# Six trial write-backs on GpSimd between the first tile and the second in a nanmax over 65536 rows

## The chip, the core and the metric

The kernel runs on one core of one Trainium2 chip. The metric is the device time of one execution in microseconds (us). Before the change it is 1251.34 us, the median of 3 runs (1251.2 to 1251.43).

Engines are named as in the profile: DVE is VectorE, ACT is ScalarE, POOL is GpSimd, SP is SyncE, which here only issues DMAs. TensorE does nothing.

## The reference

```python
def setup_inputs():
    batch, seq, dim = 32, 2048, 2048
    x = np.random.randn(batch, seq, dim).astype(np.float32)
    mask = np.random.rand(batch, seq, dim) < 0.1
    x[mask] = np.nan
    return {"x": x, "axis": -1}

def reference(x, axis):
    return np.nanmax(x, axis=axis).astype(np.float32)
```

512 MiB of float32 with a tenth of NaNs are read, and the largest number of each of the 65536 rows of 2048 elements is written, 256 KiB in all.

## The kernel before, in words

The maximum of a row must pass over NaNs. The kernel does that on the upper 16 bits of each number, before DVE takes an ordinary maximum:

1. **Load.** SP loads a tile of up to seven rows for each of the 128 partitions (up to 128x14336 elements, 7 MiB) into one of three buffers `xt` (L469; the very first load is L264).
2. **Key.** ACT reads the upper half of each float as an int16, and writes a 16-bit key for it into one of three buffers `kt` of 6144 elements (L277). The key saturates, so that NaNs come out as an ordinary pattern of a very small number.
3. **Write-back.** POOL (in the later part of the program at times ACT) turns the key back and writes it over the upper half in `xt`: `key * -1 + TOP` by one `tensor_scalar` with two operations, a packed uint16 source and an int16 target of stride two (L287).
4. **Maximum.** DVE reduces the cleaned rows of the tile to one number each (L294).

At five places POOL also looks for rows in which every element was a NaN (L309 and L323), and at the end SP stores the results (L556).

A table, `TILES`, gives for each of the 74 tiles how it is cut in loads, keys, write-backs and maxima, in units of 512 elements. The first tile, number 0, has one row for each partition (4 units, 128x2048). The next 46 have 28 units: one load, keys and write-backs of 7, 9 and 12 units, maxima of 16 and 12 units. Tile *n* uses buffer `xt[n % 3]`, and its load waits until DVE has finished tile *n* - 3. Keys go round through the buffers `kt[1]`, `kt[2]`, `kt[0]`, and so on: tile 0's key and the first key of tile 1 share `kt[1]`, the second key of tile 1 is the first use of `kt[2]`, and the third the first use of `kt[0]`.

No scheduler moves anything. The instructions stand on each engine in the order in which the Python loop issues them, and each engine works in that order. `Order.add` gives each instruction the semaphore waits for the events that it is handed, without those that are already implied, and returns its own event. `kfree[k]` holds, for each key buffer, the last write-back that read it; a key into that buffer waits for it. For tiles listed in `EARLY`, the last key of the tile waits for the next buffer's write-backs too.

In the rows of the two programs below, `kt_60`, `kt_61` and `kt_62` are `kt[0]`, `kt[1]` and `kt[2]`; `xt` is the first buffer of rows, `xt_58` and `xt_59` are the other two.

Of the kernel before, what the change touches and what calls it, by code (L numbers as in the profile page):

```python
# [9 lines left out]
D = 2048  # L10
# [73 lines left out]
TOP = 0x7F7F  # L84
# [8 lines left out]
def joints(keys, backs, reds):  # L93


    parts = []
    pieces = []
    at = end = step = 0
    for n, wait in backs:
        end += n  # L100
        while at < end:
            at += keys[step]
            step += 1
        if wait is None or wait >= 0:
            parts.append((end - n, end, wait is not None, step + (wait or 0), len(pieces)))
        pieces.append(n)
    needs = []
    done = 0
    for n in map(abs, reds):
        over = [i for i, p in enumerate(parts) if p[0] < done + n and p[1] > done]  # L110
        done += n
        pools = [i for i in over if not parts[i][2]]
        acts = sorted((i for i in over if parts[i][2]), key=lambda i: parts[i][3])
        if pools and acts and parts[pools[-1]][3] > parts[acts[-1]][3]:
            acts = []
        needs.append(pools[-1:] + acts[-1:])
    pairs = {}
    for need in needs:
        if len(need) == 2 and all(sum(i in n for n in needs) == 1 for i in need):
            both = tuple(parts[i][4] for i in need)  # L120
            for i in both:
                pairs[i] = both
    return pairs
# [62 lines left out]
def kernel(  # L186
# [15 lines left out]
    nc = tc.nc  # L202
    P = nc.NUM_PARTITIONS
    f32, i32 = mybir.dt.float32, mybir.dt.int32
    i16, u16 = mybir.dt.int16, mybir.dt.uint16
    ALU = mybir.AluOpType
# [29 lines left out]
    kts = [sing.tile([P, KEYS], u16, name=f"kt{i}") for i in range(NKEYS)]  # L236
# [21 lines left out]
    order = Order(nc)  # L258
    heads = []
    for number in range(HEADS):  # L260
        (c,) = TILES[number][0]
        gi, base = place[number]
        to = xts[number][:, 0 : c * Q]
        head = nc.sync.dma_start(  # L264
            out=dataclasses.replace(to, dep_tracking_offset=to.offset + P * WIDE * D),
            in_=groups[gi][0][:, base : base + c * Q],
# [4 lines left out]
    with tc.tile_critical() as section:  # L271

        def act(deps, pair=None, **kw):
            return order.add(
                "act",
                nc.scalar,
                lambda: nc.scalar.activation(**kw),  # L277
                deps,
                lane=pair,
                joint=pair is not None,  # L280
            )
# [51 lines left out]
        kfree = [{} for _ in range(NKEYS)]  # L333
# [45 lines left out]
        def freed(*ks):  # L379

            uses = [(back, then, e) for k in ks for back, ((_, then), e) in kfree[k].items()]
            counts = [e[1] for _, _, e in uses if e[0] == "pool"]
            deps = []
            for back, then, e in uses:
                if back == "act" and order.count["act"] >= then:
                    e = ("act", then)
                if back != "pool" or e[0] == "pool" or all(v < then for v in counts):
                    deps.append(e)
            return deps
# [39 lines left out]
        def find_part(i):  # L429
            gi, lo, hi = spans[i]  # L430
            first = groups[gi][2]
            acc = accs[:, first + lo : first + hi]
            deps = [done_at[PARTS[i][2]]]
            if PARTS[i][3] == "dve":
                ready[i] = find("dve", nc.vector, deps, acc, None)
            else:
                none = late[:, 0 : hi - lo]
                ready[i] = find("pool", nc.gpsimd, deps, acc, none)

        for number, (loads, chunks, reds) in enumerate(TILES):  # L440
            keys = [k for ks, _ in chunks for k in ks]
            fresh = {}
            step = 0
            for ks, bs in chunks:
                assert sum(ks) * Q <= KEYS
                assert sum(ks) == sum(b[0] if isinstance(b, tuple) else b for b in bs)
                fresh[step] = int(sum(ks) * Q)
                step += len(ks)
            backs = [b for _, bs in chunks for b in bs]
            backs = [b if isinstance(b, tuple) else (b, None) for b in backs]  # L450
            assert sum(loads) == sum(keys) == sum(b for b, _ in backs) == sum(map(abs, reds))
            pairs[number] = joints(keys, backs, reds)
            for i, part in enumerate(PARTS):
                if part[3] == number:
                    find_part(i)
            gi, base = place[number]
            xg = groups[gi][0]
            xt, before = xts[number % BUFS], free[number % BUFS]
            assert number < BUFS or state["tile"] > number - BUFS
            landed = []  # L460
            at = 0
            for c in loads:
                c = int(c * Q)
                e = order.add(
                    "sp",
                    nc.sync,
                    lambda: heads[number]
                    if number < HEADS
                    else nc.sync.dma_start(  # L469
                        out=xt[:, at : at + c], in_=xg[:, base + at : base + at + c]  # L470
                    ),
                    before + lanes[turn],
                    lane=f"load{turn}",
                    step=16,
                )
                lanes[turn] = [e]
                turn = (turn + 1) % LANES
                landed.append((at, at + c, e))
                at += c
            end = at  # L480
            at = lo = part = 0
            for step, c in enumerate(keys):
                c = int(c * Q)
                here = [l for a, b, l in landed if a < at + c and b > at]
                kold = []
                if used + fresh.get(step, 0) > KEYS:
                    key = (key + 1) % NKEYS
                    used = 0
                    assert all(h[3] != key for h in held)
                    assert all(q[2] != key for v in half.values() for q in v)  # L490
                    kold = freed(key, (key + 1) % NKEYS) if number in EARLY and at + c == end else freed(key)
                    kfree[key] = {}
                e_key = act(
                    kold + here,
                    out=kts[key][:, used : used + c],
                    in_=xt[:, at : at + c].bitcast(i16)[:, 1::2],
                    func=ACT.Prelu,
                    bias=EDGE,
                    scale=-1.0,
                    alpha=float(TOP - LOW) / (EDGE - NAN),  # L500
                )
                used += c
                at += c
                for h in held:
                    h[-1] -= 1
                for h in [h for h in held if h[-1] <= 0]:
                    held.remove(h)
                    write(*h[:-1], "act")
                while backs and lo + backs[0][0] * Q <= at:
                    n, wait = backs.pop(0)  # L510
                    n = int(n * Q)
                    kp = kts[key][:, used - (at - lo) : used - (at - lo) + n]
                    if wait is not None and wait > 0:
                        held.append([number, lo, lo + n, key, kp, e_key, part, wait])
                    else:
                        who = "pool" if wait is None else "act" if wait == 0 else "dve"
                        write(number, lo, lo + n, key, kp, e_key, part, who)
                    lo += n
                    part += 1
                if number == len(TILES) - 1 and at == end:  # L520
                    for h in held:
                        write(*h[:-1], "act")
                    held.clear()
                maxima(number)
            assert lo == end
        assert state["tile"] == len(TILES)
        for i, part in enumerate(PARTS):
            if not isinstance(part[3], int):
# [4 lines left out]
        n = len(whole)  # L533
# [73 lines left out]
```

## Time and profile before

| what | value |
|---|---|
| median of 3 runs | 1251.34 us |
| the profiled execution | 1251.19 us |
| its span | 1249.5 us |
| DVE busy | 1109.5 us, 184 instructions |
| ACT busy | 979.2 us, 285 instructions |
| POOL busy | 1160.0 us, 255 instructions |
| DMA queue of the loads busy | 99.5% of the span |

The span runs from the first to the last recorded instruction of the profiled execution; the time beside it includes some 1.7 us around it. Busy times of the engines overlap. For a queue of DMAs, busy is the share of the 16 DMA engines' time that its packets took. An idle time in brackets stands before the instruction that ended it, with the engine that released that instruction.

### The profile page before, as it was taken

To read this page: it belongs to the slowest core of one execution; us is meant where nothing else is said; L and a number is where in the kernel's file an instruction comes from. 1 tells how busy PE (TensorE), PEld (TensorE's weight loads), DVE (VectorE), ACT (ScalarE), POOL (GpSimd) and SP (SyncE) were. 2 spreads that over 40 slices of the span, in tenths; PEclk is the share of its full clock that TensorE was granted. 3 is DMA by queue.
4 is the path that set the end of the run, shared out by engine and by line. 5 is a ranking of instruction groups with operands and counts; after the bars stand their busy time and mean duration, and the time that the engine had idled before them with its cause. 6 is when DMAs were issued, how large, how long until landed. Compare 5 with 4: busy or idle time off the path is not lost.

```text
span 1249.5 us, 915 instructions
## 1 busy us (share of the span) xinstructions
DVE 1109.5 (89%) x184; ACT 979.2 (78%) x285; POOL 1160.0 (93%) x255
## 2 busy tenths in 40 slices
DVE  0888889888889888889888888988898999999999
ACT  3777777777777777777777777799877789999998
POOL 2999999999999999999999999967999988999988
DMA  9999999999999999999999999999999999999997
GB/s 415 441 428 424 441 441 435 417 441 441 435 426 432 441 439 431 422 441 441 433 428 431 441 439 431 422 441 441 435 426 432 441 435 432 424 435 427 431 426 316
DMA packets 16950, 537.19 MB, mean 430 GB/s; under 512 B 2608, under 2 KB 2608, under 8 KB 5296
## 3 DMA queue, kind: packets, MB, share of 16 engines
q1 hardware_dynamic: 16944, 537.14, 99.5%
q14 instruction: 6, 0.05, 0.0%
HBM read 536.87 MB, written 0.26 MB: 430 GB/s over the span
## 4 chain that ended last, share of the span: by engine, by line
POOL 37%; DVE 29%; DMA 25%; ACT 8%; issue 1%; SPq 0%
POOL xt L287 37%; DVE acc L294 29%; DMA xt<-in_x_dram 25%; ACT kt L277 7%; ACT xt L277 2%; POOL late L309 0%; POOL acc L323 0%; SPq L264 0%; SPq L469 0%; DVE acc L301 0%; SPq L602 0%; SPq L271 0%
## 5 line engine op out<-in xcount | busy, mean ns | idle before, releaser
L287 POOL TENSOR_SCALAR xt<-kt 128x3584 int16<-128x3584 uint16 (+12 forms) x240 | 1155.0, 4812 | 83.4 <-ACT kt L277 68.2
L294 DVE TENSOR_REDUCE acc<-xt 128x3 f32<-128x6144 f32 (+4 forms) x183 | 1109.3, 6115 | 137.6 <-POOL xt L287 130.7
L277 ACT ACTIVATE kt<-xt 128x3584 uint16<-128x3584 int16 (+11 forms) x251 | 913.8, 3677 | 263.2 <-DMA xt<-in_x_dram 224.8
L277 ACT ACTIVATE xt<-kt 128x512 int16<-128x512 uint16 (+10 forms) x32 | 67.8, 2117 | 0.7
L309 POOL TENSOR_SCALAR late<-acc 128x112 int32<-128x112 f32 (+1 forms) x5 | 2.8, 559 | 0.4
L323 POOL TENSOR_TENSOR acc<-acc,late 128x112 int32<-128x112 int32 (+1 forms) x5 | 2.0, 397 | 0.4
L277 ACT ACT_TABLE_LOAD x1 | 1.3, 1283 | 1.3 <-SPq L271 1.3
L329 POOL MEMSET scalars<- 128x1 f32 x1 | 0.1, 98 | 0.9 <-SPq L271 0.9
L588 POOL MEMSET const-float32-0.0<- 128x1 f32 x1 | 0.1, 99 | 0.2 <-issue 0.2
L277 ACT ACTIVATE scalars<-scalars 128x1 f32<-128x1 f32 x1 | 0.2, 202 | 0.0
L301 DVE SCALAR_TENSOR_TENSOR acc<-acc 128x7 f32<-128x7 f32 x1 | 0.2, 166 | 0.0
L588 POOL MEMSET const-bfloat16-1.0<- 128x1 bf16 x1 | 0.1, 102 | 0.0
L588 POOL MEMSET const-uint8-127<- 128x1 uint8 x1 | 0.1, 102 | 0.0
L588 POOL MEMSET const-float32-1.0<- 128x1 f32 x1 | 0.1, 99 | 0.0
## 6 DMA issues: line engine op xcount, KB each, us to landing
xt<-in_x_dram SPq DMA_DIRECT2D x62, 7168.0 KB, 22.6
xt<-in_x_dram SPq DMA_DIRECT2D x6, 1536.0 KB, 24.9
xt<-in_x_dram SPq DMA_DIRECT2D x2, 4096.0 KB, 19.8
xt<-in_x_dram SPq DMA_DIRECT2D x2, 3584.0 KB, 25.7
xt<-in_x_dram SPq DMA_DIRECT2D x2, 3072.0 KB, 26.7
xt<-in_x_dram SPq DMA_DIRECT2D x1, 5632.0 KB, 20.3
xt<-in_x_dram SPq DMA_DIRECT2D x2, 2816.0 KB, 24.9
xt<-in_x_dram SPq DMA_DIRECT2D x2, 2560.0 KB, 26.0
```

The source lines that it names most:

```text
L277: lambda: nc.scalar.activation(**kw),
L287: lambda: nc.gpsimd.tensor_scalar(**kw),
L294: return order.add("dve", nc.vector, lambda: do(**kw), deps)
L301: lambda: engine.scalar_tensor_tensor(out=acc, in0=acc, scalar=0.0, in1=acc, op0=ALU.mult, op1=ALU.add),
L309: lambda: engine.tensor_scalar(out=none, in0=acc, scalar1=LEAST, scalar2=float(0x00400000), op0=ALU.is_lt, op1=ALU.mult,),
L323: lambda: engine.tensor_tensor(out=bits, in0=bits, in1=none, op=ALU.add),
L329: e_top = order.add("pool", nc.gpsimd, lambda: nc.gpsimd.memset(top, EDGE), [])
L588: nc = _bacc.Bacc("TRN2", target_bir_lowering=False, num_devices=1)
```

## The change

Behind the code of tile 0, and so ahead of everything of tile 1 on ACT, POOL and DVE, it adds the following:

- a memset on DVE that fills all 6144 elements of `kt[0]` with the constant 1;
- six instructions on POOL, each over 1024 elements from `kt[0]`, each into one of three ranges of `kt[2]` in the pattern of a write-back (int16, stride two). The first and the fifth have the write-back's two operations. The second and the sixth copy int16 to int16, the third copies uint16 to int16, the fourth multiplies only. The first four read 1024 packed elements; the fifth and sixth read every second of 2048;
- a wait of the first trial for the memset, and of each further trial for the one before it;
- an entry for the last trial in `kfree[0]` and `kfree[2]`, so that the next key into each of these buffers waits for it.

What the trials write is never read: the keys of tile 1 go over it.

```diff
             assert lo == end
+            if number == 0:
+                n = D // 2
+                e = order.add("dve", nc.vector, lambda: nc.vector.memset(kts[0], 1), [])
+                packed = kts[0][:, 0:n]
+                apart = kts[0][:, n : 3 * n][:, 1::2]
+                kt = kts[2].bitcast(i16)
+                g = nc.gpsimd
+                kw = dict(op0=ALU.mult, op1=ALU.add, scalar1=-1.0, scalar2=float(TOP))
+                trials = (
+                    lambda to: g.tensor_scalar(out=to[:, 1::2], in0=packed, **kw),
+                    lambda to: g.tensor_copy(out=to[:, 1::2], in_=packed.bitcast(i16)),
+                    lambda to: g.tensor_copy(out=to[:, 1::2], in_=packed),
+                    lambda to: g.tensor_single_scalar(
+                        out=to[:, 1::2], in_=packed, scalar=-1.0, op=ALU.mult
+                    ),
+                    lambda to: g.tensor_scalar(out=to[:, 1::2], in0=apart, **kw),
+                    lambda to: g.tensor_copy(out=to[:, 1::2], in_=apart.bitcast(i16)),
+                )
+                deps = [e]
+                for i, trial in enumerate(trials):
+                    to = kt[:, 2 * n * (i % 3) : 2 * n * (i % 3 + 1)]
+                    e = order.add("pool", g, lambda: trial(to), deps)
+                    deps = [e]
+                kfree[0] = {"pool": ((0, 0), e)}
+                kfree[2] = {"pool": ((0, 0), e)}
         assert state["tile"] == len(TILES)
```

POOL's queue at its start, as the instructions stand there with their waits; `xt<-kt_61 128x2048` is the write-back of tile 0, and `xt_58` belongs to tile 1:

```order
 L329 MEMSET scalars 128x1
 L287 ISA
 L287 TENSOR_SCALAR xt<-kt_61 128x2048 [waits order_act]
+L535 TENSOR_SCALAR kt_62<-kt_60 128x1024 [waits order_dve]
+L536 COPY kt_62<-kt_60 128x1024 [waits order_pool]
+L537 CAST kt_62<-kt_60 128x1024 [waits order_pool]
+L538 TENSOR_SCALAR kt_62<-kt_60 128x1024 [waits order_pool]
+L541 TENSOR_SCALAR kt_62<-kt_60 128x1024 [waits order_pool]
+L542 COPY kt_62<-kt_60 128x1024 [waits order_pool]
 L287 TENSOR_SCALAR xt_58<-kt_61 128x3584 [waits order_act]
 L287 TENSOR_SCALAR xt_58<-kt_62 128x4608 [waits order_act]
```

The six trials stand between the write-back of tile 0 and the first of tile 1, and nothing else has moved on POOL.

ACT's queue at its start, with the keys of tile 0, of tile 1 (from `xt_58`) and the first of tile 2 (from `xt_59`):

```order
 L277 ACT_TABLE_LOAD
 L277 ACTIVATE scalars<-scalars 128x1 [waits order_pool]
 L277 ACTIVATE kt_61<-xt 128x2048 [waits order_load0]
 L277 ACTIVATE kt_61<-xt_58 128x3584 [waits order_load1]
-L277 ACTIVATE kt_62<-xt_58 128x4608
+L277 ACTIVATE kt_62<-xt_58 128x4608 [waits order_pool]
 L277 ACTIVATE kt_60<-xt_58 128x6144 [waits order_pool]
 L277 ACTIVATE kt_61<-xt_59 128x3584 [waits order_load2]
```

The second key of tile 1 had no wait and now waits for POOL, that is for the last trial. On DVE the memset stands between the maximum of tile 0 and the first of tile 1. SP's queue is the same in both.

## The prediction

> **What bounds the kernel now.** I read the page's totals first, to see which resource is full.
>
> ```profile
> span 1249.5 us, 915 instructions
> DVE 1109.5 (89%) x184; ACT 979.2 (78%) x285; POOL 1160.0 (93%) x255
> DMA  9999999999999999999999999999999999999997
> DMA packets 16950, 537.19 MB, mean 430 GB/s; under 512 B 2608, under 2 KB 2608, under 8 KB 5296
> q1 hardware_dynamic: 16944, 537.14, 99.5%
> ...
> xt<-in_x_dram SPq DMA_DIRECT2D x62, 7168.0 KB, 22.6
> ```
>
> Three engines are busy for 78 to 93%, but the queue of the loads is busy for 99.5% of the span. The 512 MiB of input come in one unbroken stream, and while it is unbroken no engine's lateness shows at the end. So the question about any added work is not how long it takes but whether it makes a load start so late that the stream runs dry. A gap there is paid in full: the last 180 us are one chain on DVE, which hangs on the loads' landing.
>
> ```profile
> 1032.66 22.16 DMA xt<-in_x_dram
> ...
> 1068.18 125.79 DVE acc L294 x32
> 1193.98 52.93 DVE acc L294 x24
> ```
>
> These pieces of the chain that ended last say it: a load, and (after one key and two write-backs) DVE to the end.
>
> Next I read the timeline of the first 75 us, where the change sits. Columns: start, duration, engine and operation, idle time before it.
>
> ```profile
> 7.49 2.46 POOL L287 TENSOR_SCALAR xt<-kt 128x2048 int16<-128x2048 uint16 x1 [6.02 <-ACT kt L277]
> 9.99 2.29 DVE L294 TENSOR_REDUCE acc<-xt 128x1 f32<-128x2048 f32 x1 [9.99 <-POOL xt L287]
> ...
> 22.37 7.12 ACT L277 ACTIVATE kt<-xt 128x3584 uint16<-128x3584 int16 x2 [14.96 <-DMA xt<-in_x_dram]
> 25.64 16.70 POOL L287 TENSOR_SCALAR xt<-kt 128x3584 int16<-128x3584 uint16 x3 [15.68 <-ACT kt L277]
> 29.84 5.32 ACT L277 ACTIVATE kt<-xt 128x6144 uint16<-128x6144 int16 x1 [0.35 <-POOL xt L287]
> 35.24 15.14 DVE L294 TENSOR_REDUCE acc<-xt 128x4 f32<-128x8192 f32 x2 [22.97 <-POOL xt L287]
> 39.28 7.12 ACT L277 ACTIVATE kt<-xt 128x3584 uint16<-128x3584 int16 x2 [4.11 <-DMA xt<-in_x_dram]
> ...
> 56.26 7.12 ACT L277 ACTIVATE kt<-xt 128x3584 uint16<-128x3584 int16 x2 [4.15 <-DMA xt<-in_x_dram]
> ...
> 73.16 3.19 ACT L277 ACTIVATE kt<-xt 128x3584 uint16<-128x3584 int16 x1 [4.08 <-DMA xt<-in_x_dram]
> ```
>
> The reader is to see two things. POOL sits idle for 15.68 us before 25.64: that is the hole into which the trials go. And ACT starts a new tile at 39.28, 56.26 and 73.16, each time released by a landing, so a full tile takes the stream about 16.94 us.
>
> Then the loads. SP issues the load of a tile when DVE has finished the tile three before it in the same buffer. The wait list of SP's queue and two looks at the timeline show this:
>
> ```profile
> SPq L469 <- DVE acc L294: 1151.4, 70, 37.8
> ```
>
> ```profile
> 12.30 0.33 SPq L469 DMA_DIRECT2D xt<-in_x_dram  x1
> ```
>
> ```profile
> 50.41 0.33 SPq L469 DMA_DIRECT2D xt<-in_x_dram  x1
> ```
>
> The load of tile 3 goes out at 12.30, right behind DVE's first reduce, and that of tile 4 at 50.41, behind the two reduces of tile 1 (35.24 + 15.14 = 50.38). At 50.41 the stream still has tile 3 to deliver until about 56.24, so the queue is 5.83 us ahead. A load also needs time of its own before its bytes flow. The first load of all, issued into an empty queue, gives that:
>
> ```profile
> L264 SPq DMA_DIRECT2D xt<-in_x_dram x1: 368/368/368, 0.7 to 0.7; - x1
> ...
> DMA to landing us min/median/max: 4.7/4.7/4.7
> ```
>
> It carries 1 MiB, which at the page's mean of 430 GB/s takes 2.44 us, so about 2.26 us of the 4.7 are fixed. **Tile 4's load may therefore be late by 5.83 - 2.26 = 3.57 us before the stream stops.** That is the cover.
>
> **The change part by part.** It removes nothing. It adds one memset of 6144 elements on DVE, six instructions on POOL in a chain, a wait of the first trial for DVE, and a wait of ACT's key into buffer 2 (4608 elements, tile 1) for the last trial. In before, that key follows the first one without a stop inside the 7.12 us. The key into buffer 0 already waits for a later POOL instruction. SP's queue and the DMAs get nothing new: the load of tile 3 waits for DVE's first reduce, which stands ahead of the memset. Behind DVE's memset stands the reduce of 35.24; behind the trials stands the write-back of 25.64; behind the waiting ACT key stand the third key of tile 1 and then tile 2's.
>
> For the durations I use the groups of instructions kept apart by shape (busy us and mean ns of one behind the first bar):
>
> ```profile
> L294 DVE TENSOR_REDUCE acc<-xt 128x3 f32<-128x6144 f32 x62 | 405.6, 6543 | 1.2 <-POOL xt L287 1.2
> L287 POOL TENSOR_SCALAR xt<-kt 128x6144 int16<-128x6144 uint16 x51 | 359.1, 7041 | 4.6 <-ACT kt L277 0.6
> ...
> L287 POOL TENSOR_SCALAR xt<-kt 128x3584 int16<-128x3584 uint16 x57 | 239.0, 4193 | 24.6 <-ACT kt L277 21.9
> ...
> L287 POOL TENSOR_SCALAR xt<-kt 128x1024 int16<-128x1024 uint16 x6 | 8.0, 1335 | 0.6 <-ACT kt L277 0.2
> ...
> L309 POOL TENSOR_SCALAR late<-acc 128x112 int32<-128x112 f32 x4 | 2.4, 591 | 0.3
> ...
> L323 POOL TENSOR_TENSOR acc<-acc,late 128x112 int32<-128x112 int32 x4 | 1.7, 421 | 0.3
> ...
> L309 POOL TENSOR_SCALAR late<-acc 128x57 int32<-128x57 f32 x1 | 0.4, 431 | 0.1
> L323 POOL TENSOR_TENSOR acc<-acc,late 128x57 int32<-128x57 int32 x1 | 0.3, 304 | 0.1
> ...
> L329 POOL MEMSET scalars<- 128x1 f32 x1 | 0.1, 98 | 0.9 <-SPq L271 0.9
> ```
>
> *The memset.* No row shows a memset of this size. Below it stands the 0.10 us of a 128x1 memset, above it the 6.54 us that DVE takes to pass through 6144 elements in a reduce. I take 6.54, the same engine and the same count. DVE is free from 9.99 + 2.29, and SP acts on that at 12.30; so the memset ends at 18.84 and the first trial starts at 18.89 (0.05 for the hand-over, as between 7.49 + 2.46 and 9.99).
>
> The Trainium skill (VectorE: DVE Perf Modes, section "Zero memsets can be issued as uint32 (trn2)") says that a memset takes one cycle per element whatever the dtype. By its 0.96 GHz that is an estimate of 6.4 us, and the sum would be 0.1 us lower; no row here shows one.
>
> *The trials.* Trial 1 is the write-back's own form and has a row: 1.335 us. Trial 5 is the same two operations from a source of stride two; I take the same, with nothing else in the rows to price the stride. The other four (copy, copy with a change of type, one multiplication, copy from a strided source) are forms that no row shows. The rows bound them. The write-back costs (7041 - 4193) / 2560 = 1.11 ns an element. L309, the same opcode with a compare and a multiplication, costs (591 - 431) / 55 = 2.91 ns an element and 0.27 us fixed. L323, an add of two tensors, costs (421 - 304) / 55 = 2.13 ns. So of three forms on POOL the multiply-and-add alone is quick, and everything else on this engine costs two to three times as much per element. At 1024 elements the ends are 1.34 us and 0.27 + 1024 x 2.91 / 1000 = 3.25 us. I take the upper end for these four, since they are not multiply-and-add and the dearer one-input row is the nearest that isn't.
>
> *The sum.* 2 x 1.335 + 4 x 3.25 = 15.67 us. Between two POOL instructions of which the second waits for the first lie 0.07 to 0.08 us (313.51 + 0.61 to 314.19, below), five times, so 0.40. The last trial ends at 18.89 + 15.67 + 0.40 = 34.96, and the first write-back of tile 1 starts at 35.04 in place of 25.64: **9.40 us late**. The ACT key that now waits starts at 35.0 and takes 4 us (4608 of the 8192 elements in 7.12 us), about as long as the write-back beside it, so it adds nothing of its own. Everything behind keeps its spacing, and tile 4's load goes out at 59.81. Of the 9.40 us the cover takes 3.57; **5.83 us of empty stream are left**.
>
> What follows that? Not a second gap, but not by much: POOL, behind its work, makes a tile in 16.80 us (324.37 to 341.17 below), so tile 5's load goes out at 50.41 + 9.40 + 16.80 = 76.61 and can flow at 78.87, while tile 4 lands at 73.1 + 5.8 = 78.9. From then on POOL gains 0.14 us a tile on the stream. That lateness inside the cover costs nothing, before shows itself. At 313 us POOL has 1.1 us of extra work (the first finding of empty rows):
>
> ```profile
> 313.51 0.61 POOL late L309
> ...
> 314.19 0.42 POOL acc L323
> ...
> 324.37 7.04 POOL xt L287
> ...
> 341.17 7.04 POOL xt L287
> ```
>
> ```profile
> DMA to landing us min/median/max: 21.5/22.2/22.5
> ```
>
> ```profile
> 200.00:310.00 110.00, 97.39 (x14) 79.27 (x19) 107.69 (x20) 1.00 1.00 434
> 320.00:425.00 105.00, 92.37 (x13) 78.83 (x19) 103.57 (x19) 1.00 1.00 433
> ```
>
> The first fence is from the chain, the second gives the seven loads issued between 320 and 425 us, the third two stretches (its last columns are DMA share and GB/s). Loads issued about 1.1 us later land sooner after their issue (21.5 at the least, where 22.6 is the median of the full loads in the page's list), and the stream keeps 433 GB/s. POOL heads the chain for seven tiles, until the lateness is worked off.
>
> The profiled execution took 1251.19 us (span 1249.5 and 1.7 around it), 0.15 under the median of the runs. With 5.83 it becomes 1257.0, and the median 1251.34 becomes **1257.2 us**.
>
> **The rivals.** *The hole holds everything.* If all six trials cost the write-back's 1.335 us, they end at 27.30, the write-back is 1.74 us late, the cover takes it, and the time stays 1251.3. For it: trial 1's row, and the same write pattern in all six. Against it: L309 and L323. The mechanism decides at 3.57 us of lateness, which is 9.84 us for the six together. The Trainium skill (GPSIMD Engine Reference, section "Engine selection") speaks for this rival: one-input operations on GpSimd run at roughly line rate. By its 1.2 GHz that is an estimate of 0.9 us a copy and no change of the time; the write-back's row agrees with it, L309's 2.91 ns does not.
>
> *Only some forms are dear.* Each of the four that drops from 3.25 to 1.335 takes 1.91 us off: three dear ones give +3.9 (1255.3), two +2.0 (1253.3), one +0.1.
>
> *All are dearer.* All six at 3.25 us give 19.5 us and +9.7 (1261.0). If the write's 1.11 ns came on top of the 2.91 in the four, each would cost 4.4 us, which gives +10.4 (1261.7).
>
> *The memset is short.* At its lower bound it returns 6.44 us, the lateness of the forecast falls to 2.96, and the cover hides all: 1251.3. At four elements a step (4.9 us saved) +0.9 remain.
>
> *The trials give something back.* Nothing in the program gets shorter, and the stream cannot go faster for it; I leave 0.02 for faster.
>
> **How the numbers follow.** Forecast with three or four dear forms, or dearer ones: 0.72. Two dear: 0.10. The hole holds it (none or one dear): 0.13. Short memset: 0.03. Faster: 0.02. A measurement of this kernel can tell about 0.2%, here 2.5 us, from no change; two dear forms and the hidden cases fall inside that, so same 0.26, slower 0.72. The range leaves out the hidden cases and faster (0.18): from two dear forms, 1253.3, to the upper bound of the unknown forms, 1261.7.
>
> **What would show it.** In the changed kernel the memset should stand at 12.3 with about 6.5 us; trials 1 and 5 with 1.33 us, the other four with about 3.2; the write-back at 35.0 with ACT's key as its neighbour; tile 4's first key near 79.0 in place of 73.16; a chain in which the trials stand ahead of tile 4's load; and loads that land under 22 us after issue for some 25 tiles. Wrong is the forecast if the copies take the write-back's time, if a strided source costs by itself, or if the stream stops earlier or later than 3.57 us of lateness allow.

## The result, and the profile after

The changed kernel takes 1253.40 us (median of 18 runs, 1252.75 to 1254.14) against 1251.34 us (18 runs, 1251.2 to 1251.54). The ratio is 1.0016, with a 95% interval of 1.0010 to 1.0022. So it is slower by 2.06 us, where 5.9 were forecast, and the time lies 0.1 us above the low end of the range. Its runs also differ more among themselves: by 1.39 us, where those of before differ by 0.34 (by 0.53 to 0.70 in the larger sets measured beside the experiments). This spread lies in the kernel itself: the spans of the 18 runs go from 1250.7 to 1252.1 us.

The profiled execution of the changed kernel took 1252.75 us, the lowest of the 18. The opening lines of its page:

```profile
span 1250.7 us, 922 instructions
DVE 1114.8 (89%) x185; ACT 979.4 (78%) x285; POOL 1170.1 (94%) x261
...
q1 hardware_dynamic: 16944, 537.14, 99.5%
```

DVE has 5.3 us more, the memset, and POOL 10.1 us more, the trials; the span is 1.2 us longer. Most of the added work on POOL has vanished into the idle time. The share of the DMA queue doesn't show what happened to the remainder: it reads 99.5% as before, because a packet that takes longer counts as busy (the packets of the loads took 1244.6 us for each DMA engine, 1243.6 in before).

The timeline from the memset to tile 1's write-backs:

```profile
13.66 5.18 DVE L528 MEMSET kt<- 128x6144 uint16 x1 [1.23 <-issue]
18.92 1.33 POOL L535 TENSOR_SCALAR kt<-kt 128x1024 int16<-128x1024 uint16 x1 [8.81 <-DVE kt L528]
20.31 1.32 POOL L536 COPY kt<-kt 128x1024 int16<-128x1024 int16 x1
21.70 1.33 POOL L537 CAST kt<-kt 128x1024 int16<-128x1024 uint16 x1
...
23.11 3.07 POOL L538 TENSOR_SCALAR kt<-kt 128x1024 int16<-128x1024 uint16 x1
26.27 1.33 POOL L541 TENSOR_SCALAR kt<-kt 128x1024 int16<-128x1024 uint16 x1
27.66 1.32 POOL L542 COPY kt<-kt 128x1024 int16<-128x1024 int16 x1
29.01 4.04 ACT L277 ACTIVATE kt<-xt 128x4608 uint16<-128x4608 int16 x1 [3.30 <-POOL kt L542]
29.06 105.06 POOL L287 TENSOR_SCALAR xt<-kt 128x3584 int16<-128x3584 uint16 x19
```

The memset ends at 18.84, to the hundredth where the sum had it. The hundredth is luck: DVE's first reduce ended 0.15 us later than in before (10.14 + 2.29), and from there the memset needed 6.41 us and not 6.54. Then the sum fails: only the single multiplication is dear (3.07 us); copies, with or without a change of type, and the strided source cost the 1.32 to 1.33 us of the write-back. The first write-back starts at 29.06 in place of 25.64, 3.42 us late instead of 9.40 (0.15 us of it by which this execution runs behind from its first load on). By the prediction's own cover of 3.57 us that should have cost nothing. What it did cost shows in the keys that begin a tile, in the same timeline:

```profile
39.42 7.12 ACT L277 ACTIVATE kt<-xt 128x3584 uint16<-128x3584 int16 x2 [0.82 <-DMA xt<-in_x_dram]
...
56.39 7.12 ACT L277 ACTIVATE kt<-xt 128x3584 uint16<-128x3584 int16 x2 [1.01 <-DMA xt<-in_x_dram]
...
73.86 7.12 ACT L277 ACTIVATE kt<-xt 128x3584 uint16<-128x3584 int16 x2 [1.67 <-DMA xt<-in_x_dram]
...
90.75 7.12 ACT L277 ACTIVATE kt<-xt 128x3584 uint16<-128x3584 int16 x2 [1.73 <-DMA xt<-in_x_dram]
...
108.44 7.12 ACT L277 ACTIVATE kt<-xt 128x3584 uint16<-128x3584 int16 x2 [2.60 <-DMA xt<-in_x_dram]
...
125.82 7.12 ACT L277 ACTIVATE kt<-xt 128x3584 uint16<-128x3584 int16 x2 [3.16 <-DMA xt<-in_x_dram]
```

Each starts when its load has landed. The steps are 16.97, **17.47**, 16.89, **17.69** and **17.38** us for tiles 3 to 7, where 16.9 is a load's own time. In before they are 16.98, 16.90, 16.98, 16.93 and 17.03 (the two starts beyond those shown above are here):

```profile
90.14 7.12 ACT L277 ACTIVATE kt<-xt 128x3584 uint16<-128x3584 int16 x2 [4.16 <-DMA xt<-in_x_dram]
...
107.07 7.12 ACT L277 ACTIVATE kt<-xt 128x3584 uint16<-128x3584 int16 x2 [4.11 <-DMA xt<-in_x_dram]
...
124.10 7.12 ACT L277 ACTIVATE kt<-xt 128x3584 uint16<-128x3584 int16 x2 [4.21 <-DMA xt<-in_x_dram]
```

So tiles 4, 6 and 7 are held up; from tile 3 to tile 7 it takes 69.43 us in place of 67.84, and then it is over. Not all of this reaches the end: tile 7 lands 1.72 us later than in before, the last load 0.96 us later. Before has small hold-ups of its own further on (0.44 us at tile 24, 0.33 at tile 56), which do not appear here. The load of tile 4 goes out at this point of the timeline:

```profile
53.85 0.33 SPq L469 DMA_DIRECT2D xt<-in_x_dram  x1
```

That is 3.44 us later than before, and still 2.5 us ahead of tile 3's landing. The trace has an event for each of the 16 DMA engines when its share of a load has landed. For tile 4 these lie between 72.96 and 73.83, a spread of 0.87 us; in before they lie between 72.67 and 73.14, 0.47 us. Some engines lost next to nothing, others half a microsecond. The packets show where it is lost. A full load is 128 packets of 57344 bytes, eight for each engine, which take about 2.12 us each. The first 16 of tile 4's load begin between 55.6 and 56.1 us, as each engine is done with tile 3, and ten of them take over 2.2 us, up to 2.67. Of the next 16 all but two take 2.12 or little more. In before none between 53 and 60 us takes over a tenth more than 2.12.

### The profile page after: what moved, and what is told of

It is laid out like the page before. It is cut to its first block, busy times and chain, and to the rows that moved or that the text cites. A ratio compares the mean times of both kernels' runs of the same rounds, so it can differ in the third digit from the quotient of the medians.

```text
span 1250.7 us, 922 instructions
## 1 busy us (share of the span) xinstructions
DVE 1114.8 (89%) x185; ACT 979.4 (78%) x285; POOL 1170.1 (94%) x261
## 3 DMA queue, kind: packets, MB, share of 16 engines
q1 hardware_dynamic: 16944, 537.14, 99.5%
## 4 chain that ended last, share of the span: by engine, by line
POOL 59%; DVE 19%; DMA 14%; ACT 7%; issue 1%; SPq 0%
POOL xt L287 58%; DVE acc L294 19%; DMA xt<-in_x_dram 14%; ACT kt L277 5%; ACT xt L277 2%; DVE kt L528 0%; POOL kt L538 0%; POOL kt L535 0%; POOL kt L541 0%; POOL kt L537 0%; POOL kt L536 0%; POOL kt L542 0%; POOL late L309 0%; POOL acc L323 0%; SPq L469 0%
## 5 line engine op out<-in xcount | busy, mean ns | idle before, releaser
L535 POOL TENSOR_SCALAR kt<-kt 128x1024 int16<-128x1024 uint16 x1 | 1.3, 1329 | 8.8 <-DVE kt L528 8.8
L528 DVE MEMSET kt<- 128x6144 uint16 x1 | 5.2, 5178 | 1.2 <-issue 1.2
L309 POOL TENSOR_SCALAR late<-acc 128x112 int32<-128x112 f32 (+1 forms) x5 | 2.8, 559 | 0.4
L538 POOL TENSOR_SCALAR kt<-kt 128x1024 int16<-128x1024 uint16 x1 | 3.1, 3071 | 0.1
L541 POOL TENSOR_SCALAR kt<-kt 128x1024 int16<-128x1024 uint16 x1 | 1.3, 1327 | 0.1
L536 POOL COPY kt<-kt 128x1024 int16<-128x1024 int16 x1 | 1.3, 1322 | 0.1
L542 POOL COPY kt<-kt 128x1024 int16<-128x1024 int16 x1 | 1.3, 1319 | 0.1
```

Source lines behind the costliest of these rows:

```text
L309: lambda: engine.tensor_scalar(out=none, in0=acc, scalar1=LEAST, scalar2=float(0x00400000), op0=ALU.is_lt, op1=ALU.mult,),
L528: e = order.add("dve", nc.vector, lambda: nc.vector.memset(kts[0], 1), [])
L535: lambda to: g.tensor_scalar(out=to[:, 1::2], in0=packed, **kw),
L536: lambda to: g.tensor_copy(out=to[:, 1::2], in_=packed.bitcast(i16)),
L538: lambda to: g.tensor_single_scalar(out=to[:, 1::2], in_=packed, scalar=-1.0, op=ALU.mult),
L541: lambda to: g.tensor_scalar(out=to[:, 1::2], in0=apart, **kw),
```

## The experiments

Two theories were set against each other in the first runs. **A**: the trials make tile 1's write-back late, that makes loads late, and loads that are issued less than some 3 to 4 us ahead of the stream's end lose time before the stream is dry. **B**: the memset, ACT's new wait or the trials themselves cost, whatever the lateness. Edits are to the changed kernel unless said otherwise. Intervals are 95% intervals of the ratio to before on the same chip.

**e1_no_single**, without the multiplication:

```diff
-                    lambda to: g.tensor_single_scalar(
-                        out=to[:, 1::2], in_=packed, scalar=-1.0, op=ALU.mult
-                    ),
```

> Theory A (the time comes from late loads: the trials make tile 1's first write-back late, so the loads of tiles 4 to 7 are issued late and the DMA engines run dry in turn): without the single multiplication the last trial ends 3.15 us earlier, the write-back is 0.3 us late, no load comes within 4.5 us of the stream's end, and the time is 1251.3 to 1251.6 us. Theory B (the memset, the wait of ACT or the mere presence of the trials costs, whatever the lateness): memset, wait and five trials remain, so at least 1.5 of the 2.06 us remain, 1252.8 or more.

Measured 1251.58 us, ratio 1.0002 (0.9993 to 1.0011). With memset, wait and five trials still there, 1.8 of the 2.06 us are gone. B falls, as far as it blames the memset, ACT's wait or the other five trials; the multiplication itself is left for the next run.

**e2_early**, all six trials in time:

```diff
-                e = order.add("dve", nc.vector, lambda: nc.vector.memset(kts[0], 1), [])
-                packed = kts[0][:, 0:n]
-                apart = kts[0][:, n : 3 * n][:, 1::2]
+                packed = kts[1][:, 0:n]
+                apart = kts[1][:, 0 : 2 * n][:, 1::2]
...
-                deps = [e]
+                deps = []
...
-                kfree[0] = {"pool": ((0, 0), e)}
```

> All six trials, the single multiplication too, read tile 0's key and need no memset; they should run from about 10.1 to 20.2 us, inside POOL's idle time. Theory A: nothing is late, 1251.3 to 1251.5 us. Theory B, as far as it holds the trials or ACT's wait to blame: about 1253.

Measured 1251.28 us, ratio 0.9999 (0.9990 to 1.0008). Three rows of its timeline:

```profile
14.13 3.06 POOL L537 TENSOR_SCALAR kt<-kt 128x1024 int16<-128x1024 uint16 x1
...
18.66 1.32 POOL L541 COPY kt<-kt 128x1024 int16<-128x1024 int16 x1
...
25.69 9.60 POOL L287 TENSOR_SCALAR xt<-kt 128x3584 int16<-128x3584 uint16 x2 [5.72 <-ACT kt L277]
```

The same six instructions, the dear one too, end at 19.98 and leave POOL idle for 5.72 us. Work that is over before it is waited for is free.

**e3_memset_only**, no trials, and the next key into `kt[0]` waits for the memset alone (three lines added to the kernel before):

```diff
             assert lo == end
+            if number == 0:
+                e = order.add("dve", nc.vector, lambda: nc.vector.memset(kts[0], 1), [])
+                kfree[0] = {"dve": ((0, 0), e)}
         assert state["tile"] == len(TILES)
```

> The memset alone, no trials and no wait of ACT for them. Theory A: 1251.3 to 1251.5 us. Theory B, as far as it holds the memset to blame (a start-up of the code, a shifted DVE): about 1253.

Measured 1251.51 us, ratio 1.0001 (0.9992 to 1.0010). The memset as such does not make the 2 us.

**e4_single_x3**, the multiplication three times:

> Three single multiplications in place of one: 2 x 3.15 us more lateness, 9.7 us in all, about what the prediction had (9.4). Theory A with a soft threshold: tile 4's load goes out at about 60.1 and lands some 20 us later, 7.0 us later than before, and the next loads lose about 1 us more: 1259.3 us, within 1258.3 to 1260.3. The prediction's own cover of 3.57 us, taken as exact: 1251.3 + 9.7 - 3.6 = 1257.4. Theory B: 1253 to 1254.

Measured 1259.62 us, ratio 1.0066 (1.0053 to 1.0078): theory A's 1259.3, and not the 1257.4 of the prediction's cover. Its timeline has tile 4's load and the keys of tiles 4, 5 and 6:

```profile
59.83 0.33 SPq L469 DMA_DIRECT2D xt<-in_x_dram  x1
```

```profile
79.00 7.12 ACT L277 ACTIVATE kt<-xt 128x3584 uint16<-128x3584 int16 x2 [0.81 <-DMA xt<-in_x_dram]
...
95.90 7.12 ACT L277 ACTIVATE kt<-xt 128x3584 uint16<-128x3584 int16 x2 [0.90 <-DMA xt<-in_x_dram]
...
114.95 7.12 ACT L277 ACTIVATE kt<-xt 128x3584 uint16<-128x3584 int16 x2 [3.15 <-DMA xt<-in_x_dram]
```

This load goes out at 59.83, later than tile 3's landing at 56.13: the stream is dry. It starts tile 4 at 79.00, 5.84 us later than before, which is what the prediction made of this lateness (5.83); so its arithmetic of a dry stream holds. But then tile 6 needs 19.05 us in place of 16.9. The gap is not paid once: POOL is still late, the next loads come with the same small margin, and one of them loses 2.1 us more.

**e5_dve_delay**, the kernel before with an extra reduce and no trials, so that a load is late without POOL being late:

```diff
+                if number == 1 and state["red"] == 1:
+                    dve(
+                        [],
+                        nc.vector.tensor_reduce,
+                        out=late[:, 0:1].bitcast(f32),
+                        in_=xt[:, 0:3136].bitcast(f32),
+                        axis=mybir.AxisListType.X,
+                        op=ALU.max,
+                    )
                 e = dve(
```

> The kernel before, with one extra reduce of 3136 elements on DVE (about 3.4 us) ahead of tile 1's last reduce, and no trial: tile 4's load goes out as late as in the changed kernel (53.8), tile 5's about 1.6 us late, tile 6's on time, because DVE has 1.8 us of slack a tile and POOL has 0.14. Theory A: only load 4 loses its 0.5 to 0.7 us, nothing is lost at tiles 6 and 7, and the time is 1251.8 to 1252.2. If the loss were made by the trials themselves and not by the late load: 1251.3.

Measured 1252.80 us, ratio 1.0011 (1.0002 to 1.0020). From its timeline:

```profile
43.98 3.41 DVE L294 TENSOR_REDUCE late<-xt 128x1 f32<-128x3136 f32 x1
...
53.87 0.33 SPq L478 DMA_DIRECT2D xt<-in_x_dram  x1
```

```profile
74.94 7.12 ACT L277 ACTIVATE kt<-xt 128x3584 uint16<-128x3584 int16 x2 [5.81 <-DMA xt<-in_x_dram]
...
91.83 7.12 ACT L277 ACTIVATE kt<-xt 128x3584 uint16<-128x3584 int16 x2 [4.07 <-DMA xt<-in_x_dram]
...
108.75 7.12 ACT L277 ACTIVATE kt<-xt 128x3584 uint16<-128x3584 int16 x2 [4.10 <-DMA xt<-in_x_dram]
```

A late load alone costs, with nothing on POOL; that is the cause shown apart. The place of the loss was as expected (tile 4 alone, then steps of 16.89 and 16.92), its size was not: 1.72 us in this execution, against 0.54 for a load issued at the same moment in the changed kernel. Here too the first 16 packets of tile 4 are the long ones, up to 2.99 us. What a load in this stretch loses is not fixed by when it is issued.

**e6_act_tile2**, one write-back of tile 2 on ACT, so that POOL would catch up:

```diff
-    + [([28], [([7], [7]), ([9], [9]), ([12], [12])], [16, 12])] * 46
+    + [([28], [([7], [7]), ([9], [9]), ([12], [12])], [16, 12])]
+    + [([28], [([7], [7]), ([9], [(9, 0)]), ([12], [12])], [16, 12])]
+    + [([28], [([7], [7]), ([9], [9]), ([12], [12])], [16, 12])] * 44
```

> The changed kernel, with the second write-back of tile 2 (4608 elements) on ACT in place of POOL, so that POOL catches up 5.3 us at once. Theory A: load 4 is as late as in the changed kernel and loses 0.5 to 0.7 us, loads 6 and 7 are issued in good time and lose nothing: 1251.8 to 1252.2. A hard cover that the trials pass only once (loss at load 4 alone): no change from the changed kernel, 1253.4.

Measured 1255.05 us, ratio 1.0029 (1.0018 to 1.0041). Both guesses missed, because the edit didn't do what it was for:

```profile
46.52 5.33 ACT L279 ACTIVATE xt<-kt 128x4608 int16<-128x4608 uint16 x1
51.88 12.34 ACT L279 ACTIVATE kt<-xt 128x6144 uint16<-128x6144 int16 x3
...
57.28 57.43 POOL L289 TENSOR_SCALAR xt<-kt 128x6144 int16<-128x6144 uint16 x10 [7.54 <-ACT kt L279]
```

The write-back on ACT holds up ACT's own third key, and POOL waits 7.54 us for it. Tile 6's load goes out 1.8 us later than in the changed kernel, 2.7 us ahead of the stream's end, and loses 2.6 us. It fits A, but it was no test of the repair.

**e7_single_768**, the multiplication over 768 elements:

```diff
-                        out=to[:, 1::2], in_=packed, scalar=-1.0, op=ALU.mult
+                        out=to[:, 1:1536:2], in_=packed[:, 0:768], scalar=-1.0, op=ALU.mult
```

> The single multiplication over 768 elements in place of 1024: 0.7 us less lateness, 2.7 us. Theory A with a soft threshold near 3 us ahead of the first engine to finish: tile 4's load goes out about 2.8 us ahead of it, so part of the loss remains, 1251.6 to 1252.6. A hard cover of 3.57 us: 1251.3.

Measured 1252.48 us, ratio 1.0010 (1.0000 to 1.0019). All 11 runs (1252.0 to 1253.23) lie above all of before's (1251.09 to 1251.64). The keys of tiles 3 to 5:

```profile
56.28 7.12 ACT L277 ACTIVATE kt<-xt 128x3584 uint16<-128x3584 int16 x2 [1.84 <-DMA xt<-in_x_dram]
...
73.29 7.12 ACT L277 ACTIVATE kt<-xt 128x3584 uint16<-128x3584 int16 x2 [2.03 <-DMA xt<-in_x_dram]
...
91.37 3.19 ACT L277 ACTIVATE kt<-xt 128x3584 uint16<-128x3584 int16 x1 [3.31 <-DMA xt<-in_x_dram]
```

At 2.5 us of lateness, well inside the predicted cover, part of the loss is still there. But not where it was expected: tile 4's load, issued 3.35 us ahead, loses 0.09 us, and tile 5's, issued 3.55 us ahead, loses 1.16. The first 16 packets of tile 4 take 2.12 us each, those of tile 5 take 2.37 to 3.38.

**e8_forms**, five other trials in e2's place (here as lines added to the kernel before):

```diff
...
+                short = packed[:, 0:512]
+                trials = (
+                    lambda to: g.tensor_single_scalar(
+                        out=to[:, 1::2], in_=packed, scalar=-1.0, op=ALU.mult
+                    ),
+                    lambda to: g.tensor_single_scalar(
+                        out=to[:, 1:n:2], in_=short, scalar=-1.0, op=ALU.mult
+                    ),
+                    lambda to: g.tensor_single_scalar(
+                        out=to[:, 0:n], in_=packed, scalar=-1.0, op=ALU.mult
+                    ),
+                    lambda to: g.tensor_single_scalar(
+                        out=to[:, 1::2], in_=packed, scalar=1.0, op=ALU.add
+                    ),
+                    lambda to: g.tensor_copy(out=to[:, 0:n], in_=packed.bitcast(i16)),
+                )
...
```

> Five other trials in the idle time, reading tile 0's key: a single multiplication over 1024 elements, over 512, over 1024 into a packed target, a single addition over 1024, a copy over 1024 into a packed target. If one operation has a slow loop of its own: 3.07, 1.64, about 3.1 and about 3.1 us. If the loop is slow only for the stride of two in the target: the packed multiplication falls to 1.3 or less. If the copy's 1.32 us are the pace of its strided writes: the packed copy is clearly shorter, 0.9 us or less; if they are the copy's own loop: 1.3 again. All ends by 23 us, so the time is that of before.

Measured 1251.2 us in a single execution. The groups kept apart by shape, in the order of the list L533, L536, L539, L542, L545:

```profile
L533 POOL TENSOR_SCALAR kt<-kt 128x1024 int16<-128x1024 uint16 x1 | 3.1, 3061 | 0.1
L542 POOL TENSOR_SCALAR kt<-kt 128x1024 int16<-128x1024 uint16 x1 | 3.1, 3061 | 0.1
L539 POOL TENSOR_SCALAR kt<-kt 128x1024 int16<-128x1024 uint16 x1 | 2.8, 2767 | 0.1
...
L536 POOL TENSOR_SCALAR kt<-kt 128x512 int16<-128x512 uint16 x1 | 1.6, 1628 | 0.1
...
L545 POOL COPY kt<-kt 128x1024 int16<-128x1024 int16 x1 | 1.0, 1036 | 0.1
```

One operation alone, multiplication or addition, costs (3061 - 1628) / 512 = 2.80 ns an element; a packed target saves only a tenth. A packed copy takes 1.04 us, a strided one 1.32. So among these 16-bit forms the price belongs to `tensor_scalar` with one operation, not to the stride and not to whether it multiplies or adds. It is no rule that two operations are quick: L309 in before, a compare and a multiplication from float32 to int32, has two and costs 2.91 ns an element.

The last four runs ask what the loss hangs on.

**f1_mult_add0**, the same product with an addition of 0:

```diff
-                    lambda to: g.tensor_single_scalar(
-                        out=to[:, 1::2], in_=packed, scalar=-1.0, op=ALU.mult
+                    lambda to: g.tensor_scalar(
+                        out=to[:, 1::2],
+                        in0=packed,
+                        op0=ALU.mult,
+                        op1=ALU.add,
+                        scalar1=-1.0,
+                        scalar2=0.0,
                     ),
```

> The fourth trial computes the same product with an addition of 0 behind it, so that it has the write-back's two operations. Theory A: 1.33 us in place of 3.07, the write-back 1.7 us late, tile 4's load issued about 4.1 us ahead of the stream's end, at the edge of the stretch in which loads lost something (2.3 to 4.2 us ahead): 1251.3 to 1252.0 us. If the dear part is the multiplication itself and not the number of operations: 3.07 us again and 1253.4.

Measured 1251.66 us, ratio 1.0003 (0.9994 to 1.0012). From the groups and the timeline of the profiled execution, the fastest of its 11 runs (1251.40 us):

```profile
L538 POOL TENSOR_SCALAR kt<-kt 128x1024 int16<-128x1024 uint16 x1 | 1.3, 1332 | 0.1
```

```profile
51.91 0.33 SPq L469 DMA_DIRECT2D xt<-in_x_dram  x1
```

Two operations take 1.33 us where one takes 3.07. Tile 4's load goes out at 51.91, 4.34 us ahead of the stream's end, and in this trace no load of tiles 4 to 9 is held up: their steps are 16.88 to 16.98 us.

**f2_single_x2**, the multiplication twice:

> Two single multiplications: 6.5 us of lateness. Theory A: tile 4's load goes out at about 57.0, after the stream has run dry, lands 19.2 to 20 us later (2.9 to 3.8 us late), and the next two or three loads, issued 2.3 to 4.2 us ahead, lose 1 to 2 us together: 1255.2 to 1257.2 us. The hard cover of 3.57 us alone: 1254.3.

Measured 1256.61 us, ratio 1.0042 (1.0030 to 1.0055), inside A's 1255.2 to 1257.2 and 2.3 us above the hard cover's 1254.3. In its trace tile 4's load loses 2.60 us to the dry stream, and tile 6's, issued 2.44 us ahead, 2.39 more.

**f3_act_third**, e6's idea where ACT has time for it, behind its third key:

```diff
-    + [([28], [([7], [7]), ([9], [9]), ([12], [12])], [16, 12])] * 46
+    + [([28], [([7], [7]), ([9], [9]), ([12], [(4, 0), 8])], [16, 12])] * 3
+    + [([28], [([7], [7]), ([9], [9]), ([12], [12])], [16, 12])] * 43
```

> The changed kernel, with the first 2048 of the 6144 elements of the third write-back on ACT in tiles 1, 2 and 3, behind ACT's third key, so that POOL catches up at once without a wait for ACT's keys. Theory A: load 4 is issued as late as in the changed kernel (its maxima are not helped) and loses 0.5 to 1.7 us; loads 5 to 7 are issued 4.3 us or more ahead and lose nothing: 1251.9 to 1253.1. If it is not the late loads 6 and 7 that lose: 1253.4 as in the changed kernel.

Measured 1252.53 us, ratio 1.0010 (1.0001 to 1.0019): 0.87 us less than the changed kernel. The keys of tiles 4 to 7:

```profile
74.30 7.12 ACT L278 ACTIVATE kt<-xt 128x3584 uint16<-128x3584 int16 x2 [2.79 <-DMA xt<-in_x_dram]
...
91.19 7.12 ACT L278 ACTIVATE kt<-xt 128x3584 uint16<-128x3584 int16 x2 [4.06 <-DMA xt<-in_x_dram]
...
108.12 7.13 ACT L278 ACTIVATE kt<-xt 128x3584 uint16<-128x3584 int16 x2 [4.11 <-DMA xt<-in_x_dram]
...
125.12 3.19 ACT L278 ACTIVATE kt<-xt 128x3584 uint16<-128x3584 int16 x1 [4.18 <-DMA xt<-in_x_dram]
```

Tile 4 is late by 1.14 us, then the steps are 16.89, 16.93 and 17.00. The losses at tiles 6 and 7 were made by POOL's remaining lateness, and in this trace they go with it.

**f4_halves**, smaller packets for tiles 4 to 7:

```diff
-    + [([28], [([7], [7]), ([9], [9]), ([12], [12])], [16, 12])] * 46
+    + [([28], [([7], [7]), ([9], [9]), ([12], [12])], [16, 12])] * 3
+    + [([14, 14], [([7], [7]), ([9], [9]), ([12], [12])], [16, 12])] * 4
+    + [([28], [([7], [7]), ([9], [9]), ([12], [12])], [16, 12])] * 39
```

> The changed kernel, with the loads of tiles 4 to 7 each in two halves of 7168 elements, issued one behind the other, so that a DMA packet has 28 KB in place of 56 KB; the issue of the first half is as late as before. If an engine loses time because it has no next packet at hand while it moves its last one (2.12 us for 56 KB, 1.06 for 28 KB): the stretch of loads that lose shrinks by about 1 us, and the time falls to 1251.6 to 1252.6. If the loss doesn't hang on the packet: 1253 to 1254.

Measured 1253.07 us, ratio 1.0015 (1.0006 to 1.0024). The result is on the side of a loss that doesn't hang on the packet. Its trace says the same: tile 4's load, issued 2.72 us ahead, loses 1.27 us. Its first 16 packets, of 28672 bytes and 1.06 us as a rule, together take 3.7 us too long; the first 16 whole packets of tile 4 in the changed kernel took 3.1 us too long together. The guess of an engine that has no next packet at hand while it moves its last one is not borne out.

**All loads together.** From the issues and landings in the 13 traces without f4 (before, after, and the other eleven), for each load of tiles 4 to 61: how far its issue is ahead of the landing of the load before it, and how much more than 16.92 us lies between the two landings.

```
issued ahead of the last landing   loads   lost us: mean   range
4.3 us or more                       737      0.00         over 0.15 in 22 of them, at most 0.89
2.3 to 4.2 us                         15      0.99         0 to 2.56
not at all (0.4 and 3.7 us behind)     2      4.26         2.60 and 5.93
```

The last row is the plain arithmetic of a dry stream: both loads landed 19.1 us after their issue, 16.9 plus 2.2. The middle row is what the prediction didn't know. The two loads in it that were issued latest, 2.3 us ahead, lost nothing; both stand right behind a load that began in a dry stream.

In the loads of the middle row that lost over 0.4 us, the long packets are mostly the first of each engine, and in tile 6 of e4, e6 and f2 the second as well; from the fourth on they are close to 2.12 us again.

## Why the prediction was wrong

- **The bound held.** The stream of loads sets the time, work in POOL's idle time is free (e2), and a late load alone shows at the end (e5). Paid in full holds for the gaps of a dry stream: what e4 and f2 lost is still there at the last load. Of the smaller losses a part is won back: 1.2 of the 1.7 us of tile 4 in e5 are left at the last load, and 0.4 of the 1.2 us of tile 5 in e7.
- **The memset** was right in size, 6.41 us from the end of the reduce against 6.54. That its end came at 18.84 as forecast is two small errors that cancel.
- **The step that failed first is "I take the upper end for these four, since they are not multiply-and-add".** Three of the four are copies and cost 1.32 us, not 3.25; the single multiplication was near in size (3.07), but by luck: it was priced by a compare and a multiplication. The six took 9.70 us and not 15.67, and the lateness was 3.42 us and not 9.40. L309's 2.91 ns an element, a compare and a multiplication, was taken as the price of whatever is not multiply-and-add. It turned out to be near the price of one operation (2.80), and says nothing of a copy. The rival in which only one form is dear had the operations right, and gave +0.1.
- **The second step that failed is the cover, "Tile 4's load may therefore be late by 5.83 - 2.26 = 3.57 us before the stream stops".** As the moment at which the stream is dry that was right: loads issued into a dry stream land 2.2 us later than their own 16.9, against 2.26 forecast. But time is lost well before. Loads issued 3.55 and 3.28 us ahead lost 1.16 and 0.76 us, and one issued 4.13 us ahead lost 0.47, with two first packets of 3.1 and 3.6 us; in f1, where all came 4.34 us or more ahead, tiles 4 to 9 lost nothing. So the loss begins somewhere between 1.5 and 2.3 us of lateness, and not at 3.57. That is why the rival with one dear form missed the 2.06 us too.
- **A third one, "not a second gap, but not by much", was wrong as well.** POOL works its lateness off at 0.14 us a tile, so a lateness that has once used up the margin keeps several loads in the stretch where they lose: tiles 6 and 7 after tile 4 here, 2.1 us at tile 6 in e4. With the real prices the two errors pulled against each other, too much lateness and too little loss from it, which is why the time came out near the end of the range. That it fell inside is luck: the low end, 1253.3, stood for two dear forms and a cover of 3.57 us, and there was one dear form and a smaller cover.
- That lateness inside the cover costs nothing was argued from tiles 20 to 26, whose loads came 4.56 us ahead or more. The evidence stopped just short of where the loss begins.

What stays open is why the first packets of a load issued 2.3 to 4.2 us ahead sometimes take as long as any other and sometimes over a microsecond more, on some of the 16 engines and not on others. Halving the packets left most of the loss (1.8 us in f4). That this chance makes the changed kernel's runs spread over 1.4 us is likely, but was not shown, since only one execution of each kernel has a trace. The kernels with the memset but without late loads (e1, e3, f1) stand 0.2 to 0.4 us above before; their intervals hold 1, so that is left open too. Nor does a trace show the whole 2.06 us: the one of the changed kernel is of its fastest run, 1.56 us above that of before. No version beat the kernel before; e2, its equal, shows that these trials can be had for nothing.

## What to carry to other kernels

Where a stream of loads sets the time, what matters of added work is the margin with which the next load is issued; find that margin's smallest value that the trace has seen at full rate, and count everything below it as unknown and not as free. If an engine behind the loads has little slack a tile, one delay costs several times, so let another engine help it catch up, and only where that engine has nothing of its own behind it (f3 against e6). Idle time is used from its beginning: the same work was free when it started at 10 us, and cost 2 us when a memset let it start at 19.

## What the runs showed of the hardware

- On GpSimd, `tensor_scalar` with one operation took 2.3 times as long as with two: 3.07 us over 1024 elements for a multiplication, 1.33 us for the same multiplication with an addition of 0 behind it (f1). Addition alone was as dear, 3.06 us (e8). All of these were uint16 to int16.
- Copies into a stride of two took 1.32 us for 1024 elements, with int16 or uint16, from a packed or strided source, the same as multiply-and-add; into a packed target 1.04 us.
- VectorE's memset is recorded from 1.23 us after the end of the reduce ahead of it, with 5.18 us; in e3 the gap is the same. From one end to the other it is 6.41 us. The Trainium skill (VectorE: DVE Perf Modes, section "Zero memsets can be issued as uint32 (trn2)") gives one cycle per element, by its 0.96 GHz an estimate of 6.4 us. The trace agrees if the gap is counted in, and disagrees by the recorded 5.18 us alone; no run here shows which of the two the memset's own time is.
- A load issued into a dry stream landed 19.1 us after its issue, 2.2 us more than its own 16.9 (e4, f2). Loads issued 2.3 to 4.2 us ahead of the landing of the load before lost up to 2.56 us, and the time went mostly into the first packet of each DMA engine: up to 3.59 us where most packets took 2.12.
